# The state space branch's 256-column products: three products of high and low parts in place of one float32 product

## The chip, the cores and the metric

One core of one Trainium2 chip runs the whole program in one launch. The metric is the device time of that launch in microseconds (us). TensorE (PE) multiplies matrices, VectorE (DVE) and ScalarE (ACT) do the elementwise work, SyncE (SP) issues nearly all DMAs. Each engine takes its own instructions strictly in the order in which they were written for it, and waits at an instruction whose inputs, or whose buffer, are not ready.

## The reference

The model is two layers (sequence 512, width 1024, all float32). Each layer mixes tokens by three branches and then applies a gated MLP. The branch at issue is the Mamba-2 state space scan (16 heads of 64 channels in 4 groups, state 128, chunks of 128 tokens):

```python
cb = jnp.einsum('bctgn,bcsgn->bctsg', c, b)
y_diag = jnp.einsum('bctsg,bctsgh,bcsghp->bctghp', cb, decay, x)
states = jnp.einsum('bcsgn,bcsgh,bcsghp->bcghpn', b, to_end, x)
prev = chunk_prefix_states(jnp.exp(a_cum[:, :, -1])[..., None, None], states)
y_off = jnp.einsum('bctgn,bcghpn,bctgh->bctghp', c, prev, jnp.exp(a_cum))
return (y_diag + y_off).reshape(bsz, seq, nh, p)
```

For one group the heads' channels lie side by side, so `states` (B with x) and `y_off` (C with the states) are each one 128x128 by 128x256 product per chunk.

## The kernel before

All projections run as a stream of **units**. A unit is one 128x1024 tile of weights: SP loads it (`raw`), ACT casts it to the reduced type F32R (`wh`, L249), DVE forms the remainder (`wl`, L251), and PE does 24 matmuls of 512 columns with it (an F32R product is done three times: high by high, high by low, low by high, so that nearly float32 precision comes out). `wh` and `wl` have three buffers each, and the split is written three units ahead, so the cast of a unit waits until PE has finished the unit whose buffer it takes.

Everything else of the branches is written as Python generators (`side`), each resumed between units by `tick`, at the `yield`s it names. Their small matmuls go through `mm` and `transpose`, and after each small one `follow` puts one of the unit's 512-column matmuls. PE's order is the written one; ACT's and DVE's order, and the buffers, are set by a scheduler that reads the whole program at build time.

```python
def follow():
    if large:
        o, l, r, start, stop = large.popleft()
        PE.matmul(o, lhsT=l, rhs=r, start=start, stop=stop)     # L183

def mm(o, l, r, start, stop):
    PE.matmul(o, lhsT=l, rhs=r, start=start, stop=stop)         # L186
    follow()
```

A unit's matmuls that do not follow a small one are issued at L178. The names below: `xdt`, `xD`, `xe` are x times its step, its skip weight and its decay to the chunk's end (L833 to L836); `bt` is B transposed (L845); `cb` the masked product of C and B (L850); `M` the decay times `cb` (ACT L894 and L895, DVE L896); `prev` the running state (L873 to L877); `sy` the chunk's output, `jk` its square. `cx`, `cv`, `xbc` are the causal convolution and SiLU of a projection (DVE L771, ACT L773, DVE L775 three times, ACT L778, DVE L779). `th` and `mg` belong to the branch gates (DVE L918, ACT L919, DVE L943 and L945).

`ssd_group` runs once per group, four groups in two layers. In six steps, one per unit, it forms `M` for chunk 0 to 3 (steps 0 to 3) and does `chunk` for chunk 0 to 3 (steps 2 to 5). `chunk` issues four 64-column products of `M` with `xdt`, the product of C with `prev` (not for chunk 0), and the product of B with `xe` (not for chunk 3); DVE then makes the next `prev` from it. The next chunk, one unit later, needs that `prev`.

Of the kernel before, what the change touches and what calls it, by code (L numbers as in the profile page):

```python
# [12 lines left out]
F32R = mybir.dt.float32r  # L13
# [7 lines left out]
P = 128  # L21
# [115 lines left out]
def hybrid_decoder(ctx: ExitStack, tc: tile.TileContext, ins, out):  # L137
# [6 lines left out]
    def nm(s):  # L144
        ids[0] += 1
        return f"{s}_{ids[0]}"
# [10 lines left out]
    def big(shape, dt=F32, n="b"):  # L157
        return big_p.tile(shape, dt, tag="b", name=nm(n))
# [7 lines left out]
    def mx():  # L166
        return psum_p.tile([P, 512], F32, tag="ps", name=nm("mx"))

    V, A, PE = nc.vector, nc.scalar, nc.tensor
# [10 lines left out]
# [9 lines that stand above are left out]
    def transpose(o, i, idn):  # L189
        PE.transpose(o, i, idn)  # L190
        follow()
# [6 lines left out]
    def f(ap):  # L198
        return ap.bitcast(F32)
# [88 lines left out]
    def blk(c):  # L288
        return slice(c * P, (c + 1) * P)
# [514 lines left out]
    def bc4(ap):  # L804
        return ap.unsqueeze(2).to_broadcast([P, 4, 64])

    def ssd_group(l, g, dec, ch, zw, yh, yl):
        dt, acu, acr, e, dte = dec
        pc, rw = pcs[l], rows[l]
        bT, cT, x0, x1 = ch  # L810
        xg = big([P, 4, P], F32R, n="xg")
        V.tensor_mul(xg, f(acr).unsqueeze(1).to_broadcast([P, 4, P]),
                     own64[:, 4 * g:4 * g + 4].unsqueeze(2).to_broadcast([P, 4, P]))
        yield 1

        def hs(t, c):
            return t[:, c * 16 + 4 * g:c * 16 + 4 * g + 4]


        xdt, xd, xe = [], [], []  # L820
        for cc in range(2):
            o = mx()
            for c in range(2):
                for i, x in enumerate((x0, x1)):
                    transpose(o[:, 256 * c + P * i:256 * c + P * i + P], x[:, blk(2 * cc + c)], ident)
            td, tD, te = big([P, 2, 256], n="xdt"), big([P, 2, 256], n="xD"), big([P, 2, 256], n="xe")
            for c in range(2):
                ov = o[:, 256 * c:256 * c + 256].rearrange("p (h d) -> p h d", h=4)

                def v4(t):  # L830
                    return t[:, c].rearrange("p (h d) -> p h d", h=4)

                V.tensor_mul(v4(td), ov, bc4(hs(dt, 2 * cc + c)))  # L833
                V.tensor_mul(v4(tD), ov, bc4(rw[:, 32 + 4 * g:36 + 4 * g]))  # L834
                if 2 * cc + c < 3:
                    V.tensor_mul(v4(te), ov, bc4(hs(dte, 2 * cc + c)))  # L836
                xdt.append(td[:, c])
                xd.append(tD[:, c])
                xe.append(te[:, c])
        yield 1  # L840
        o = mx()
        for c in range(3):
            transpose(o[:, blk(c)], bT[:, blk(c)], ident)
        bt = big([P, 384], n="bt")
        A.copy(bt, o[:, :384])  # L845
        o = mx()
        for c in range(4):
            mm(o[:, blk(c)], bT[:, blk(c)], cT[:, blk(c)], True, True)
        cb = big([P, 4, P], n="cb")
        V.tensor_mul(cb, o.rearrange("p (c t) -> p c t", c=4), tri.unsqueeze(1).to_broadcast([P, 4, P]))  # L850
        ss = sml([P, 4], n="sss")
        ys = []

        def chunk(c, mt, prev):
            yd = mx()
            for h in range(4):
                mm(yd[:, 64 * h:64 * h + 64], mt[:, h], xdt[c][:, 64 * h:64 * h + 64], True, True)
            if c:
                mm(yd[:, 256:512], cT[:, blk(c)], prev, True, True)
            if c < 3:  # L860
                so = mx()
                mm(so[:, :256], bt[:, blk(c)], xe[c], True, True)
            y = big([P, 256], n="sy")
            V.tensor_add(y, yd[:, :256], xd[c])
            if c:
                t1 = big([P, 4, 64], n="t1")
                V.tensor_mul(t1, yd[:, 256:512].rearrange("p (h d) -> p h d", h=4), bc4(hs(e[:, 0], c)))
                V.tensor_add(y, y, t1.rearrange("p a b -> p (a b)"))
            nx = None
            if c < 3:  # L870
                nx = big([P, 256], n="prev")
                if c == 0:
                    V.tensor_copy(nx, so[:, :256])  # L873
                else:
                    V.tensor_mul(nx.rearrange("p (h d) -> p h d", h=4), prev.rearrange("p (h d) -> p h d", h=4),
                                 bc4(hs(e[:, 2], c)))
                    V.tensor_add(nx, nx, so[:, :256])  # L877
            V.scalar_tensor_tensor(y, y, hr[:, c:c + 1], zw[c], ALU.mult, ALU.mult)
            jk = big([P, 256], n="jk")
            A.activation(jk, y, AF.Square, accum_out=ss[:, c:c + 1])  # L880
            ys.append(y)
            return nx

        yield 1
        prev = None
        mts = []
        for c in range(6):
            if c < 4:
                sg = mx()
                mm(sg, own_c[:, c], xg.rearrange("p a b -> p (a b)"), True, True)  # L890
                mt = big([P, 4, P], n="M")
                for h in range(4):
                    j = 16 * c + 4 * g + h
                    A.activation(mt[:, h], sg[:, blk(h)], AF.Relu, bias=acu[:, j:j + 1], scale=-1.0)  # L894
                A.activation(mt, mt, AF.Exp, scale=-1.0)  # L895
                V.tensor_mul(mt, mt, cb[:, c:c + 1].to_broadcast([P, 4, P]))  # L896
                mts.append(mt)
            if c > 1:
                prev = chunk(c - 2, mts[c - 2], prev)
            yield 1  # L900
        V.tensor_scalar(ss, ss, 1.0 / 256.0, EPS, ALU.mult, ALU.add)
        ro = sml([P, 4], n="sro")
        rsqrt(ro, ss, 4)
        for c in range(4):
            A.activation(ys[c], ys[c], AF.Copy, scale=ro[:, c:c + 1])
        yield 2
        for i in range(2):
            o = mx()
            for c in range(4):
                transpose(o[:, blk(c)], ys[c][:, blk(i)], ident)  # L910
            split(yh[2 * g + i], yl[2 * g + i], o, pc[:, O_SNW + 2 * g + i:O_SNW + 2 * g + i + 1])
# [65 lines left out]
    for l in range(depth):  # L977
# [28 lines left out]
        for m in range(KD):  # L1006
            o = pp()
# [8 lines left out]
        for j in range(KF + 1):  # L1016
# [5 lines left out]
            if j:  # L1022
                i, og, ov = last
                s = big([P, T], n="fs")
                conv_silu(og, 3, lambda t: cw[:, 3 * i + t:3 * i + t + 1], cw[:, 66 + i:67 + i], s)()
                V.tensor_mul(s, s, ov)
                h, lo = big([P, T], F32R, n="hh"), big([P, T], F32R, n="hl")
# [7 lines left out]
        for m in range(KD):  # L1035
            o = pp()
            for k in range(KF):
# [3 lines left out]
                s = blk(idx % 8)  # L1041
# [89 lines left out]
```

## Time and profile before

| | |
|---|---|
| time, median of 3 runs | 2322.52 us (2321.18 to 2324.29) |
| the profiled execution | 2325.6 us, its span 2323.8 us |
| PE busy | 2300.8 us (99%) |
| DVE busy | 1420.4 us (61%) |
| ACT busy | 917.6 us (39%) |
| chain that ended last | PE 98%, DVE 1% |
| granted TensorE clock, mean | 0.995 |

The span runs from the first to the last instruction of the profiled execution; the time around it is what the launch adds. A busy share counts time in which the engine has an instruction at work. The chain that ended last is followed back from the last instruction, at each step to what released it.

### The profile page before, as it was taken

To read this page: it belongs to the slowest core of one execution; us is meant where nothing else is said; L and a number is where in the kernel's file an instruction comes from. 1 tells how busy PE (TensorE), PEld (TensorE's weight loads), DVE (VectorE), ACT (ScalarE), POOL (GpSimd) and SP (SyncE) were. 2 spreads that over 40 slices of the span, in tenths; PEclk is the share of its full clock that TensorE was granted. 3 is DMA by queue.
4 is the path that set the end of the run, shared out by engine and by line. 5 is a ranking of instruction groups with operands and counts; after the bars stand their busy time and mean duration, and the time that the engine had idled before them with its cause. 6 is when DMAs were issued, how large, how long until landed. Compare 5 with 4: busy or idle time off the path is not lost.

```text
span 2323.8 us, 27417 instructions
## 1 busy us (share of the span) xinstructions
PE 2300.8 (99%) x10776; PEld 1903.1 (82%) x10776; DVE 1420.4 (61%) x2527; ACT 917.6 (39%) x1503; POOL 0.2 (0%) x4
## 2 busy tenths in 40 slices
PE   8999999999999999999999999999999999999997
PEld 7888878888888888888888888788888888888886
DVE  5467548687865566654335764686888556665533
ACT  5354423445443333332244444234454433333321
POOL 0000000000000000000000000000000000000000
PEclk9999999999999999999999999999999999999998
DMA  5322222222223333333333222222222233323331
GB/s 182 105 77 82 73 64 87 78 72 73 82 73 100 92 99 95 96 100 94 97 91 100 83 82 73 71 84 73 73 73 82 82 95 96 97 94 100 98 93 54
DMA packets 58512, 204.21 MB, mean 88 GB/s; under 512 B 7152, under 2 KB 7824, under 8 KB 58384
## 3 DMA queue, kind: packets, MB, share of 16 engines
q1 hardware_dynamic: 57808, 201.42, 28.8%
q8 instruction: 84, 1.38, 0.2%
q10 hardware_dynamic: 576, 1.05, 0.1%
q14 instruction: 44, 0.36, 0.1%
HBM read 200.35 MB, written 2.10 MB: 87 GB/s over the span
## 4 chain that ended last, share of the span: by engine, by line
PE 98%; DVE 1%; ACT 0%; DMA 0%; issue 0%; DVEq 0%; SPq 0%; ACTq 0%
PE pp L178 77%; PE pp L183 11%; PE mx L186 8%; PE mx L190 2%; DVE wl L251 0%; DVE x L1069 0%; DVE cv L775 0%; DMA x<-in_xT 0%; DVE xD L834 0%; DVE th L918 0%; DVE th L943 0%; DVE xdt L833 0%; DVE xe L836 0%; ACT cx L778 0%; ACT L350 0%
## 5 line engine op out<-in xcount | busy, mean ns | idle before, releaser
L249 ACT CAST wh<-raw 128x1024 fp32r<-128x1024 f32 x374 | 393.1, 1051 | 952.7 <-PE pp L178 727.9
L251 DVE TENSOR_TENSOR wl<-raw,wh 128x1024 fp32r<-128x1024 f32 x374 | 457.4, 1223 | 355.6 <-ACT wh L249 350.1
L178 PE MATMUL pp<-xh,wl 128*128 128x512 f32 x1582 | 617.7, 390 | 0.0
L178 PE MATMUL pp<-xl,wh 128*128 128x512 f32 x1556 | 607.0, 390 | 0.0
L178 PE MATMUL pp<-xh,wh 128*128 128x512 f32 x1504 | 587.8, 391 | 0.0
L178 PEld LDWEIGHTS pp<-xh,wl 128*128 128x128 f32 x1582 | 297.7, 188 | 63.5 <-issue 1.0
L178 PEld LDWEIGHTS pp<-xl,wh 128*128 128x128 f32 x1556 | 293.1, 188 | 60.5 <-issue 0.5
L178 PEld LDWEIGHTS pp<-xh,wh 128*128 128x128 f32 x1504 | 283.3, 188 | 60.4 <-DVE wl L251 1.5
L183 PE MATMUL pp<-xh,wh 128*128 128x512 f32 x304 | 148.3, 488 | 0.0
L178 PE MATMUL pp<-hh,wl 128*128 128x512 f32 x352 | 136.9, 389 | 0.0
L178 PE MATMUL pp<-hh,wh 128*128 128x512 f32 x352 | 136.9, 389 | 0.0
L178 PE MATMUL pp<-hl,wh 128*128 128x512 f32 x352 | 136.9, 389 | 0.0
L771 DVE TENSOR_TENSOR cx<-pp,rstdB 128x512 f32<-128x512 f32 x76 | 52.3, 689 | 121.1 <-PE pp L178 121.0
L183 PE MATMUL pp<-xl,wh 128*128 128x512 f32 x252 | 124.6, 495 | 0.0
L183 PE MATMUL pp<-xh,wl 128*128 128x512 f32 x226 | 111.4, 493 | 0.0
L178 PE MATMUL pp<-wh,xh 128*128 128x512 f32 x245 | 96.3, 393 | 7.9 <-ACT wh L249 7.9
L178 PE MATMUL pp<-wh,xl 128*128 128x512 f32 x264 | 103.4, 392 | 0.0
L778 ACT ACTIVATE cx<-cv 128x512 f32<-128x512 f32 x76 | 48.1, 632 | 139.6 <-DVE cv L775 138.8
L178 PE MATMUL pp<-wl,xh 128*128 128x512 f32 x258 | 101.2, 392 | 0.5 <-DVE wl L251 0.5
L178 PE MATMUL pp<-wh,xr 128*128 128x512 f32 x255 | 78.7, 389 | 0.0
L178 PEld LDWEIGHTS pp<-hl,wh 128*128 128x128 f32 x352 | 66.1, 188 | 13.8
L178 PEld LDWEIGHTS pp<-hh,wl 128*128 128x128 f32 x352 | 66.1, 188 | 13.7
(275 smaller groups left out, 3542.6 us busy)
## 6 DMA issues: line engine op xcount, KB each, us to landing
raw<-in_wall SPq DMA_DIRECT2D x374, 512.0 KB, 3.6
x<-in_xT SPq DMA_DIRECT2D x8, 256.0 KB, 6.0
out_dram<-x ACTq DMA_DIRECT2D x4, 256.0 KB, 2.3
out_dram<-x SPq DMA_DIRECT2D x4, 256.0 KB, 2.5
cosR<-in_rope SPq DMA_DIRECT2D x2, 256.0 KB, 4.6
sinR<-in_rope SPq DMA_DIRECT2D x2, 256.0 KB, 4.8
amask<-in_amask SPq DMA_DIRECT2D x1, 256.0 KB, 5.3
levf<-in_lev SPq DMA_DIRECT2D x1, 224.0 KB, 3.7
```

The source lines that it names most:

```text
L178: PE.matmul(o, lhsT=l, rhs=r, start=start, stop=stop)
L183: PE.matmul(o, lhsT=l, rhs=r, start=start, stop=stop)
L186: PE.matmul(o, lhsT=l, rhs=r, start=start, stop=stop)
L190: PE.transpose(o, i, idn)
L249: A.copy(h, r)
L251: V.tensor_sub(lo, r, f(h))
L771: V.tensor_mul(x, o, rstdB)
L778: A.activation(x, v, AF.Tanh)
```

## The change

The operands of the two 256-column products become pairs of F32R tiles: a high part (ACT copy) and a low part (DVE difference). Each product becomes three. `parted` makes a pair, `three` issues the three matmuls.

```diff
+    def parted(src, n, name):
+
+        h, lo = big([P, n], F32R, n=name), big([P, n], F32R, n=name)
+        A.copy(h, src)
+        V.tensor_sub(lo, src, f(h))
+        return h, lo
+
+    def three(o, l, s, r):
+        mm(o, l[0][:, s], r[0], True, False)
+        mm(o, l[0][:, s], r[1], False, False)
+        mm(o, l[1][:, s], r[0], False, True)
...
-                xe.append(te[:, c])
+            n = 512 if cc == 0 else 256
+            h, l = parted(te.rearrange("p c d -> p (c d)")[:, :n], n, "xe")
+            xe += [(h[:, i:i + 256], l[:, i:i + 256]) for i in range(0, n, 256)]
...
-        bt = big([P, 384], n="bt")
-        A.copy(bt, o[:, :384])
+        bt = parted(o[:, :384], 384, "bt")
+        cp_ = parted(cT[:, P:], 384, "cT")
...
             if c:
-                mm(yd[:, 256:512], cT[:, blk(c)], prev, True, True)
+                three(yd[:, 256:512], cp_, blk(c - 1), prevs[-1])
             if c < 3:
                 so = mx()
-                mm(so[:, :256], bt[:, blk(c)], xe[c], True, True)
+                three(so[:, :256], bt, blk(c), xe[c])
...
+                prevs.append(parted(nx, 256, "prev"))
```

In the changed kernel's rows L810 and L811 are the copy and the difference in `parted`; L878, L881, L889, L882, L891, L893 and L895 are the old L864, L867, L875, L868, L877, L878 and L880; L909 to L911 the old L894 to L896; L933, L934 and L958 the old L918, L919 and L943.

**First place: the first group of a layer, ACT.** The rows run from the cast of one unit to the exponential of the first `M`, before the change:

```order
L249 CAST wh_4097<-raw_3907 128x1024
L773 ACTIVATE cv_4040<-cx_4038,scw_2599 128x512
L845 COPY bt_4059<-mx_4052 128x384
L249 CAST wh_4139<-raw_3964 128x1024
L778 ACTIVATE cx_4038<-cv_4040 128x512
L894 ACTIVATE M_4104<-mx_4101,acu_2905 128x128 x4
L919 ACTIVATE th_4092<-th_4092 128x512
L895 ACTIVATE M_4104<-M_4104 128x512
```

The same stretch of the changed kernel (`wh_4153` is the cast that was `wh_4139`, `M_4118` the tile that was `M_4104`):

```order
L249 CAST wh_4111<-raw_3907 128x1024
L810 CAST xe_4010<-xe_4003 128x512
L810 CAST xe_4031<-xe_4025 128x256
L249 CAST wh_4153<-raw_3964 128x1024
L773 ACTIVATE cv_4048<-cx_4046,scw_2599 128x512
L810 CAST bt_4067<-mx_4060 128x384
L810 CAST cT_4071<-xbc_3576 128x384
L778 ACTIVATE cx_4046<-cv_4048 128x512
L249 CAST wh_4205<-raw_4054 128x1024
L909 ACTIVATE M_4118<-mx_4115,acu_2905 128x128 x4
L934 ACTIVATE th_4106<-th_4106 128x512
L910 ACTIVATE M_4118<-M_4118 128x512
```

Three casts are new. The cast of one unit moved ahead of the convolution's step `cv` and of `bt`, and the cast of the next unit moved ahead of `M`; before, that one stood after the second `M`.

**The same place on DVE**, from the low part of the unit's weights to the first `M`, before:

```order
L251 TENSOR_TENSOR wl_4141<-raw_3964,wh_4139 128x1024
L775 SCALAR_TENSOR_TENSOR cv_4040<-cx_4038,scw_2599,cv_4040 128x509
L779 SCALAR_TENSOR_TENSOR xbc_4037<-cx_4038,cv_4040 128x512
L918 TENSOR_TENSOR th_4092<-pp_4045,rstdB 128x512
L918 TENSOR_TENSOR th_4135<-pp_4094,rstdB 128x512
L943 SCALAR_TENSOR_TENSOR th_4092<-th_4092,pp_4143 128x512
L896 TENSOR_TENSOR M_4104<-M_4104,cb_4070 128x512
```

and after:

```order
L251 TENSOR_TENSOR wl_4155<-raw_3964,wh_4153 128x1024
L775 SCALAR_TENSOR_TENSOR cv_4048<-cx_4046,scw_2599,cv_4048 128x511
L811 TENSOR_TENSOR bt_4068<-mx_4060,bt_4067 128x384
L775 SCALAR_TENSOR_TENSOR cv_4048<-cx_4046,scw_2599,cv_4048 128x510
L811 TENSOR_TENSOR cT_4072<-xbc_3576,cT_4071 128x384
L775 SCALAR_TENSOR_TENSOR cv_4048<-cx_4046,scw_2599,cv_4048 128x509
L864 TENSOR_TENSOR cb_4084<-mx_4075,mats 128x512
L779 SCALAR_TENSOR_TENSOR xbc_4045<-cx_4046,cv_4048 128x512
L933 TENSOR_TENSOR th_4106<-pp_4053,rstdB 128x512
L933 TENSOR_TENSOR th_4149<-pp_4108,rstdB 128x512
L251 TENSOR_TENSOR wl_4207<-raw_4054,wh_4205 128x1024
L911 TENSOR_TENSOR M_4118<-M_4118,cb_4084 128x512
```

Behind `wl_4155` stand now all three steps of the convolution, `cb`, two low parts and the low part of the next unit, before `M` comes; the first two steps and `cb` stood ahead of that `wl` before.

**Second place: the third state of a layer's second group, DVE**, before the change:

```order
L867 TENSOR_TENSOR t_920_4663<-mx_4647,dec_2899 128x256
L875 TENSOR_TENSOR prev_4666<-prev_4585,dec_2899 128x256
L868 TENSOR_TENSOR sy_4661<-sy_4661,t_920_4663 128x256
L877 TENSOR_TENSOR prev_4666<-prev_4666,mx_4658 128x256
L878 SCALAR_TENSOR_TENSOR sy_4661<-sy_4661,hr,zw_3472 128x256
L251 TENSOR_TENSOR wl_4697<-raw_4465,wh_4695 128x1024
```

and after:

```order
L775 SCALAR_TENSOR_TENSOR cv_4679<-cx_4677,scw_2599,cv_4679 128x509
L878 TENSOR_TENSOR sy_4735<-mx_4713,xD_4278 128x256
L881 TENSOR_TENSOR t_944_4737<-mx_4713,dec_2899 128x256
L889 TENSOR_TENSOR prev_4740<-prev_4651,dec_2899 128x256
L882 TENSOR_TENSOR sy_4735<-sy_4735,t_944_4737 128x256
L891 TENSOR_TENSOR prev_4740<-prev_4740,mx_4728 128x256
L893 SCALAR_TENSOR_TENSOR sy_4735<-sy_4735,hr,zw_3472 128x256
L251 TENSOR_TENSOR wl_4771<-raw_4517,wh_4769 128x1024
L811 TENSOR_TENSOR prev_4744<-prev_4740,prev_4743 128x256
```

On ACT the high part of that state (`prev_4743`) is written behind the unit's cast `wh_4769` and the convolution's tanh:

```order
L350 ACTIVATE ysh_2583<-mx_4691,pc_92 128x512
L350 ACTIVATE ysh_2584<-mx_4702,pc_92 128x512
L249 CAST wh_4769<-raw_4517 128x1024
L778 ACTIVATE cx_4677<-cv_4679 128x512
L810 CAST prev_4743<-prev_4740 128x256
```

PE needed only the sum `prev_4666` before; it needs both parts now, and the low part stands behind a 128x1024 difference.

**Third place: the second state of a layer's third group, DVE**, after the change (`scw` stands there in the first layer alone):

```order
L891 TENSOR_TENSOR prev_5311<-prev_5311,mx_5299 128x256
L911 TENSOR_TENSOR M_5277<-M_5277,cb_5073 128x512
L893 SCALAR_TENSOR_TENSOR sy_5306<-sy_5306,hr,zw_4507 128x256
L765 TENSOR_SCALAR scw_11466<-pc_95 128x80
L251 TENSOR_TENSOR wl_5341<-raw_5154,wh_5339 128x1024
L811 TENSOR_TENSOR prev_5315<-prev_5311,prev_5314 128x256
```

Here too the low part of the state stands behind a unit's `wl`. At the other states the low part stands ahead of the next `wl` or a unit's length before its use.

## Rows read from the trace of the kernel before

**Rows 1.** The page: engines' busy time, share of the span and instructions; then the chain that ended last, by engine.
```profile
PE 2300.8 (99%) x10776; PEld 1903.1 (82%) x10776; DVE 1420.4 (61%) x2527; ACT 917.6 (39%) x1503; POOL 0.2 (0%) x4
...
PE 98%; DVE 1%; ACT 0%; DMA 0%; issue 0%; DVEq 0%; SPq 0%; ACTq 0%
```

**Rows 2.** Who waited for whom, PE's own waits: total us, times, longest.
```profile
PE mx L186 <- DVE M L896: 1.4, 2, 0.7
```

**Rows 3.** PE's groups by shape: operation, output and inputs, shapes, count, busy us, mean ns of one. A float32 matmul is two instructions.
```profile
L186 PE MATMUL mx<-xe,bt 128*128 128x256 f32 x48 | 14.2, 377 | 0.0
...
L186 PE MATMUL mx<-prev,xbc 128*128 128x256 f32 x48 | 14.2, 377 | 0.0
```

**Rows 4.** From the page's costliest groups, the weight loads of the projections: mean ns of one.
```profile
L178 PEld LDWEIGHTS pp<-xh,wl 128*128 128x128 f32 x1582 | 297.7, 188 | 63.5 <-issue 1.0
```

**Rows 5.** PE's timeline at the second group's third and fourth chunk: start us, duration us, line, output and inputs, shape, instructions merged. Seven more L178 rows stand between 565.82 and 567.64, each 0.22 to 0.24 after the one before.
```profile
564.26 0.59 PE L186 MATMUL mx<-prev,xbc 128*128 128x256 f32 x2
...
564.92 0.59 PE L186 MATMUL mx<-xe,bt 128*128 128x256 f32 x2
...
565.82 0.39 PE L178 MATMUL pp<-xh,wh 128*128 128x512 f32 x1
...
567.64 0.39 PE L178 MATMUL pp<-xh,wl 128*128 128x512 f32 x1
567.87 0.33 PE L186 MATMUL mx<-xdt,M 128*128 128x64 f32 x2
...
569.68 0.59 PE L186 MATMUL mx<-prev,xbc 128*128 128x256 f32 x2
```

**Rows 6.** PE's timeline, other small matmuls between 512-column ones, in the same columns: transposes, then float32 products of 128 columns.
```profile
525.53 0.27 PE L190 MATMUL mx<-mats,xbc 128*128 128x128 f32 x1
...
525.87 0.27 PE L190 MATMUL mx<-mats,xbc 128*128 128x128 f32 x1
...
526.55 0.38 PE L186 MATMUL mx<-xbc,xbc 128*128 128x128 f32 x2
...
527.00 0.38 PE L186 MATMUL mx<-xbc,xbc 128*128 128x128 f32 x2
```

**Rows 7.** ACT's timeline ahead of the first layer's first chunk, in the same columns; in brackets the idle time before and what ended it.
```profile
507.21 1.05 ACT L249 CAST wh<-raw 128x1024 fp32r<-128x1024 f32 x1 [0.76 <-PE pp L178]
510.27 0.63 ACT L778 ACTIVATE cx<-cv 128x512 f32<-128x512 f32 x1 [2.01 <-DVE cv L775]
510.81 1.12 ACT L894 ACTIVATE M<-mx,acu 128x128 f32<-128x128 f32 x4
512.26 0.63 ACT L919 ACTIVATE th<-th 128x512 f32<-128x512 f32 x1 [0.33 <-DVE th L918]
512.80 0.61 ACT L895 ACTIVATE M<-M 128x512 f32<-128x512 f32 x1
```

**Rows 8.** DVE's timeline at the same place, and last the PE row that waited for it.
```profile
506.29 0.74 DVE L775 SCALAR_TENSOR_TENSOR cv<-cx,scw,cv 128x511 f32<-128x511 f32 x1
506.95 0.68 DVE L850 TENSOR_TENSOR cb<-mx,mats 128x512 f32<-128x512 f32 x1
507.55 0.73 DVE L775 SCALAR_TENSOR_TENSOR cv<-cx,scw,cv 128x510 f32<-128x510 f32 x1
508.29 1.23 DVE L251 TENSOR_TENSOR wl<-raw,wh 128x1024 fp32r<-128x1024 f32 x1
509.44 0.74 DVE L775 SCALAR_TENSOR_TENSOR cv<-cx,scw,cv 128x509 f32<-128x509 f32 x1
...
513.53 0.68 DVE L896 TENSOR_TENSOR M<-M,cb 128x512 f32<-128x512 f32 x1
...
514.27 0.43 PE L186 MATMUL mx<-xdt,M 128*128 128x64 f32 x2 [0.72 <-DVE M L896]
```

**Rows 9.** The second place, two units around the third state of the second group: ACT's rows, then DVE's.
```profile
561.01 0.80 ACT L773 ACTIVATE cv<-cx,scw 128x512 f32<-128x512 f32 x1
...
567.84 1.05 ACT L249 CAST wh<-raw 128x1024 fp32r<-128x1024 f32 x1 [1.87 <-PE pp L178]
...
560.72 1.23 DVE L251 TENSOR_TENSOR wl<-raw,wh 128x1024 fp32r<-128x1024 f32 x1 [0.15 <-ACT wh L249]
...
564.51 0.74 DVE L775 SCALAR_TENSOR_TENSOR cv<-cx,scw,cv 128x509 f32<-128x509 f32 x1
...
566.50 0.41 DVE L877 TENSOR_TENSOR prev<-prev,mx 128x256 f32<-128x256 f32 x1
566.83 0.47 DVE L878 SCALAR_TENSOR_TENSOR sy<-sy,hr,zw 128x256 f32<-128x256 f32 x1
```

**Rows 10.** The third place, around the second state of the third group: PE's rows, then one of ACT.
```profile
631.06 0.33 PE L186 MATMUL mx<-xdt,M 128*128 128x64 f32 x2
...
632.88 0.59 PE L186 MATMUL mx<-prev,xbc 128*128 128x256 f32 x2
...
631.03 1.05 ACT L249 CAST wh<-raw 128x1024 fp32r<-128x1024 f32 x1 [1.57 <-PE pp L178]
```

**Rows 11.** PE's timeline in the second layer where the clock fell; the last row is the sum over a stretch (from:to, length, then busy us of PE, weight loads, DVE, ACT and POOL, then PEclk, the granted clock, where 1.00 is 2.4 GHz, then DMA).
```profile
1476.66 0.63 PE L178 MATMUL pp<-xh,wh 128*128 128x512 f32 x1
...
1479.22 0.51 PE L178 MATMUL pp<-xh,wh 128*128 128x512 f32 x1
...
1474.00:1478.00 4.00, 4.00 (x13) 2.65 (x13) 0.76 (x3) 0.00 (x0) 0.00 (x0) 0.76 0.00 0
```

More of the change, by code (lines that the diff above doesn't have):

```diff
@@ L851, in ssd_group @@
         ss = sml([P, 4], n="sss")
-        ys = []
+        ys, prevs = [], []
         def chunk(c, mt, prev):
```

## The prediction

> **What bounds the kernel now.** I read the page first. PE is busy for 99% of the span, and the chain that ended last lies on it for 98%, while DVE is busy for 61% and ACT for 39% [rows 1]. So what PE saves is time, and work on ACT and DVE costs only what it makes PE wait. The view of the waits says where that is near: among PE's own waits stands the one for `M` (DVE, L896), twice, the longest 0.7 us [rows 2]. The timeline there shows PE at 514.27 after 0.72 us of idling [rows 8]; it is the first `M` of a layer, once in each layer, and so a place without any slack. Last I read the timeline around the 256-column products. Each float32 product is two instructions; there are 48 instructions for each of the two sorts [rows 3], so 24 products each, 48 in all.
>
> **What PE saves.** From 564.26 to 564.92 PE does one float32 256-column product and one 512-column product: 0.66 us. A 512-column product alone is (567.64 - 565.82) / 8 = 0.2275 us [rows 5]. The float32 product costs 0.66 - 0.2275 = 0.43 us.
>
> In its place stand three F32R products of 256 columns, and the trace has none of that shape. The bound from below is half of a 512-column product, 0.1138 us, less what such a product may have of fixed cost: I put 0.107 there. The nearest rows for a small product between large ones are a transpose, 525.87 - 525.53 - 0.2275 = 0.11, and a float32 product of 128 columns, which passes twice: (527.00 - 526.55 - 0.2275) / 2 = 0.111 a pass [rows 6]. With some hundredths of the reading of starts in hundredths, 0.12 is the bound from above. I take 0.116, so three cost 0.348 and the gain is 0.086 us a product, 48 x 0.086 = 4.1 us. The bounds give 48 x 0.07 = 3.6 and 48 x 0.11 = 5.3 us.
>
> The change also raises these products' weight loads, from 96 to 144, one for each instruction. A load takes 188 ns by its row [rows 4], while 512-column products follow each other every 0.2275 us, so those loads lie beside the products before them; I cost them at nothing, hidden by the large product that follows each small one. A small product of 0.11 us hides less than a load of 0.19; if the load behind each of the 144 small ones showed its rest, 0.188 - 0.116 = 0.07 us, that would cost 144 x 0.07 = 10.4 us. Against it speak the same transposes and 128-column passes, whose loads are as large and which cost 0.11.
>
> The Trainium skill speaks against the change here: its page "TensorE: Matmul & The Clock Gate", section "Part 3: Packing small matmuls", says that a weight load overlaps matmuls in flight only when the row group differs, and all rows here use all 128 partitions. The trace disagrees, since 188 ns of load and a whole 512-column product would not fit into 0.2275 us. By the rule each of the 48 added loads would stand open, an estimated 9 us by the 0.188 of its row; I give that no more than the chance of the costlier products below.
>
> **What ACT and DVE get.** For each group: casts and differences of `xe` (512 and 256 columns), `bt` (384, its cast in the place of the copy), `cT` (384) and three `prev` (256 each). On DVE a 256-column step takes 0.33 us from start to start (566.50 to 566.83) [rows 9], a 512-column one 0.60 (`cb`, 506.95 to 507.55), a step of the convolution 0.66 (506.29 to 506.95), a unit's `wl` 1.15 (508.29 to 509.44) [rows 8]; for 384 I estimate 0.47, between 0.33 and 0.60. A group gets some 3 us on each engine, over six units of about 7 us. Most of it is hidden behind PE's work: where I followed the written order, operands were ready 2 to 4 us early. Three places are not covered, and both layers have them in the same order, so each counts twice.
>
> **First place, `M` of the first group.** ACT's cast of the unit, released by PE at 507.21 [rows 7], now stands ahead of `cv` and `bt`, and the `wl` ahead of the three convolution steps. So DVE runs `wl` from 508.31, and behind it `cv` 509.45, the low part of `bt` 510.11, `cv` 510.58, the low part of `cT` 511.24, the last `cv` 511.71. That one ends at 512.45; it ended at 509.44 + 0.74 = 510.18 before. The tanh (L778) therefore starts at 512.50 in place of 510.27. Behind it ACT now has the next unit's cast, 1.05 us with 0.95 to the next start as instructions overlap by 0.1: that stood behind the second `M`. So the four exponents of `M` (about 1.0 us; 1.12 by their row) start at 513.98, the tanh of `th` at 514.98 and the exponential of `M` at 515.50, and it ends 0.61 us later, at 516.13 [rows 7]. DVE has done `cb`, `xbc`, two `th` and the next `wl` by 516.12, so `M` starts at 516.18, and PE, 0.74 behind it as in 513.53 to 514.27, at 516.91 [rows 8]. That is 2.64 us later than before: PE would idle for 3.4 us. Queued behind the waiting product are all later products of PE, so nothing covers it. Twice: 5.3 us. If the orders ahead slip less than I read, the least is nothing.
>
> **Second place, the third state of the second group.** Before, DVE had the sum at 566.50 + 0.41 = 566.91, and PE wanted it at 569.68 [rows 5, 9]. Its `wl` at 560.72 starts 0.17 earlier, two products' gain, at 560.55. Behind it stand now the low part of the state before, `xbc` and `cx`, until 560.55 + 1.15 + 0.33 + 2 x 0.60 = 563.2, ending 563.3; ACT's `cv`, 0.80 long, ran from 561.01 before and now ends at 564.17. Then DVE has three convolution steps with two 512-column steps between, 2 x 0.66 + 2 x 0.60 + 0.74 = 3.3, to 567.5 (565.25 before, 564.51 + 0.74). Four steps of 256 columns and the sum's own 0.41 later, the sum ends at 569.24. ACT's cast follows from 569.3 to 569.7. PE, which by then has saved 0.38 us, would take the high part at 569.30 and takes it at 569.75: 0.45 us. The low part stands behind `sy` and a `wl` of 1.15 us and ends at 571.1; PE wants it one small and one large product after the high one, at 569.75 + 0.34 = 570.09, and has it at 571.15: 1.06 us. Together 1.5, in two layers 3.0 us.
>
> **Third place, the second state of the third group.** The unit begins at U = 631.06, its cast at U - 0.03 [rows 10]. The `wl` starts some 0.03 behind the cast's end, the low part 1.15 later, and that takes 0.41, so PE can have it at about U - 0.03 + 1.05 + 0.03 + 1.15 + 0.41 + 0.05 = U + 2.66. The high product starts at U + 1.82 (631.06 to 632.88) and the low part is wanted 0.34 later, at U + 2.16: 0.5 us, twice 1.0.
>
> **The sum.** -4.1 + 5.3 + 3.0 + 1.0 = +5.2 us. The profiled execution took 2325.6 us, 3.1 (0.13%) above the median of 2322.5, its span 2323.8 and 1.8 us around it. It becomes 2330.8, on the median's basis 2327.7, rounded 2328, +0.2%. What a measurement of this kernel can tell from no change is 0.2%, 4.65 us, so the forecast lies just above that bound.
>
> **The rivals.**
>
> *The clock falls in the new gap.* In the second layer the clock was at 1.2 GHz for a while though PE did not idle, only did small products: 13 in 4 us, mean granted clock 0.76, and a 512-column product took 0.63 us, at 1479.22 still 0.51, against 0.39 [rows 11]. PE idles longer at the first place, 3.4 us, and the clock might fall too. The slow rows there reach from 1476.66 to 1479.22, and with a product on either side I put such a spell at 3.4 us; in it products come every 0.43 us, twice 0.2275, so 8 of them lose 8 x 0.2 = 1.6 us. For both layers this gives +8.4 us, 2331. It hangs on a gap as long as I work out; a much shorter one speaks against it, since with gaps of 0.7 us [rows 2] PE kept its pace.
> The Trainium skill, page "TensorE: Matmul & The Clock Gate", section "Why this matters for your kernels", warns that an idle gap between bursts of matmuls sends the clock back to half. No stretch of this trace has such a gap in the middle of the work, so it neither agrees nor disagrees.
>
> *The waits are hidden, and the time doesn't rise* (the other side). All three places rest on orders that I walked by hand with durations of before. Some rows for it: the first `M` hangs on the tanh, and if the cast of the unit is released earlier or the convolution's steps run ahead of `wl`'s release, it loses only the cast's 0.95 us. Then PE's 48 x 0.086 us stand against 2 x 0.95 and some of the 4 us of the other places: from -4.1 to +2 us, 2319 to 2324. It decides from where the first place loses under 1.5 us a layer. Below -4.65 us, faster by what can be told, it takes both no wait and products of under 0.112 us ((0.434 - 4.65 / 48) / 3): possible, but the order puts the low part of `prev` behind `wl` at two places.
>
> *Small products cost more.* If the rest of each load shows, the 10.4 us from above come on top: +15.6, 2338. If a 256-column F32R product cost a float32 pass, 0.43 / 2 = 0.217 us, three would cost 0.65 and the 48 products lose 10.4 in place of gaining 4.1: +20, 2342. The passes of 128 columns at 0.11 speak against both. Waits that I missed, at 4 to 8 us, would end at the same place: a group has 13 more tiles in the shared pool, whose reuse I followed by the order alone.
>
> **How the numbers follow.** The forecast (three places, clock kept) gets 0.38, the clock's rival 0.34, hidden waits 0.18, costlier products or more waits 0.10. The forecast's own spread, from the product's price and a place more or less, is +3 to +7 us; some four tenths of it lie below 4.65, so it gives 0.22 slower and 0.16 the same. The clock's rival gives 0.31 slower and 0.03 the same, the hidden waits 0.05 faster and 0.13 the same, the last 0.09 slower and 0.01 the same. That is faster 0.05, same 0.33, slower 0.62. The range: from 2320.5, which leaves out the lower third of the hidden waits, to 2335, which takes in the clock's rival with one more wait and leaves out most of the last; under 2 in 10 is outside.
>
> **What would show it.** The gain: in the changed trace the 256-column F32R products start 0.11 to 0.12 us before the next large one. First place: PE waits for `M` (L911), twice, some 3.4 us each, near 514 and at the same place of the second layer, and the tanh at L778 starts some 2 us later. Second and third: PE rows of L186 that wait for L810 and L811 of `prev`, 1.5 and 0.5 us a layer. The clock: the granted clock in a window behind the first place, 1.00 or about 0.5. The prediction is wrong if PE doesn't wait for L911 beyond 1.5 us, or if the small products cost over 0.13 us.

## The result and the profile after

The changed kernel takes 2337.26 us (median of 6 runs, 2336.1 to 2339.59) against 2323.08 of the kernel before (6 runs beside them): 1.0064 of it, 95% interval 1.0052 to 1.0076. That is +14.2 us, slower as forecast, but nearly three times the +5.2 of the sum and above the range. The profiled execution has a span of 2337.8 us, 14.0 more than before, so its trace holds the whole difference.

The page's engines (busy us, share of the span, instructions) and the chain by engine; [rows 1] are the same rows of before:

```profile
PE 2306.5 (99%) x10824; PEld 1907.1 (82%) x10824; DVE 1445.3 (62%) x2583; ACT 939.0 (40%) x1551; POOL 0.2 (0%) x4
...
PE 97%; DVE 2%; ACT 1%; issue 0%; DMA 0%; DVEq 0%; SPq 0%; ACTq 0%
```

PE has 48 more instructions, DVE 56 and ACT 48. DVE is busy 25 us more and ACT 21; on shares of a whole span nothing looks dangerous. PE's own waits (us in total, times, longest) show where it hurts; [rows 2] had 1.4 us for the first `M`:

```profile
PE mx L186 <- DVE M L911: 6.6, 2, 3.3
...
PE mx L186 <- DVE prev L811: 2.3, 4, 0.8
...
PE mx L190 <- DVE xD L846: 0.7, 2, 0.4
...
PE mx L186 <- ACT prev L810: 0.4, 2, 0.2
```

These waits are 8.6 us more than before. PE's timeline at the first place shows what the waits don't; [rows 8] end with the same product before, at 514.27:

```profile
512.88 0.47 PE L183 MATMUL pp<-wh,xh 128*128 128x512 f32 x1
516.66 0.69 PE L186 MATMUL mx<-xdt,M 128*128 128x64 f32 x2 [3.31 <-DVE M L911]
517.11 0.78 PE L183 MATMUL pp<-wl,xh 128*128 128x512 f32 x1
517.69 0.52 PE L186 MATMUL mx<-xdt,M 128*128 128x64 f32 x2
517.97 0.77 PE L183 MATMUL pp<-wh,xl 128*128 128x512 f32 x1
...
523.45 0.28 PE L190 MATMUL mx<-mats,xbc 128*128 128x128 f32 x1
```

Behind the gap of 3.31 us everything PE does lasts longer: a pair with a 64-column product takes 0.86 us (517.11 to 517.97), and such a pair took 0.46 before (514.51 to 514.97 in the same view). The windows of that stretch name the reason (from:to, length, busy us of PE, weight loads, DVE, ACT and POOL, then PEclk, DMA share and GB/s):

```profile
516.00:518.00 2.00, 1.34 (x6) 1.24 (x6) 2.00 (x4) 2.00 (x7) 0.00 (x0) 0.66 0.48 84
518.00:520.00 2.00, 2.00 (x8) 1.81 (x9) 2.00 (x4) 1.63 (x5) 0.00 (x0) 0.50 0.44 178
520.00:522.00 2.00, 2.00 (x7) 1.70 (x7) 1.17 (x4) 0.00 (x0) 0.00 (x0) 0.50 0.00 0
522.00:524.00 2.00, 2.00 (x9) 1.40 (x8) 1.22 (x3) 0.90 (x3) 0.00 (x0) 0.63 0.00 0
524.00:526.00 2.00, 2.00 (x13) 1.58 (x12) 1.89 (x6) 0.00 (x0) 0.00 (x0) 1.00 0.00 0
```

From 516.66 to 523.45, for 6.8 us, TensorE ran at 0.50 of its speed, 1.2 GHz. The rival of the clock came true, in both layers, and twice as long as the 3.4 us that it was given.

### The profile page after: what moved, and what is told of

It reads as the page before. It is cut to its first block, busy times and chain, and to the rows that moved or that the text cites. A ratio compares the mean times of both kernels' runs of the same rounds, so it can differ in the third digit from the quotient of the medians.

```text
span 2337.8 us, 27625 instructions
## 1 busy us (share of the span) xinstructions
PE 2306.5 (99%) x10824; PEld 1907.1 (82%) x10824; DVE 1445.3 (62%) x2583; ACT 939.0 (40%) x1551; POOL 0.2 (0%) x4
## 4 chain that ended last, share of the span: by engine, by line
PE 97%; DVE 2%; ACT 1%; issue 0%; DMA 0%; DVEq 0%; SPq 0%; ACTq 0%
PE pp L178 76%; PE pp L183 12%; PE mx L186 8%; PE mx L190 1%; DVE wl L251 1%; ACT wh L249 0%; DVE cv L775 0%; DVE x L1084 0%; DMA x<-in_xT 0%; DVE ysl L351 0%; DVE th L933 0%; DVE prev L811 0%; ACT cv L773 0%; DVE M L911 0%; DVE xe L811 0%
## 5 line engine op out<-in xcount | busy, mean ns | idle before, releaser
L178 PE MATMUL pp<-xh,wl 128*128 128x512 f32 x1564 | 610.6, 390 | 0.0
L178 PE MATMUL pp<-xl,wh 128*128 128x512 f32 x1532 | 597.6, 390 | 0.0
L178 PE MATMUL pp<-xh,wh 128*128 128x512 f32 x1482 | 579.0, 391 | 0.0
L178 PEld LDWEIGHTS pp<-xh,wl 128*128 128x128 f32 x1564 | 294.3, 188 | 62.2 <-issue 1.0
L178 PEld LDWEIGHTS pp<-xl,wh 128*128 128x128 f32 x1532 | 288.5, 188 | 59.4 <-issue 0.5
L178 PEld LDWEIGHTS pp<-xh,wh 128*128 128x128 f32 x1482 | 279.2, 188 | 59.7 <-DVE wl L251 1.5
L178 PE MATMUL pp<-hh,wl 128*128 128x512 f32 x352 | 136.9, 389 | 0.0
L178 PE MATMUL pp<-hh,wh 128*128 128x512 f32 x352 | 136.9, 389 | 0.0
L178 PE MATMUL pp<-hl,wh 128*128 128x512 f32 x352 | 136.9, 389 | 0.0
L178 PE MATMUL pp<-wh,xh 128*128 128x512 f32 x237 | 93.2, 393 | 7.6 <-ACT wh L249 7.6
L178 PE MATMUL pp<-wh,xl 128*128 128x512 f32 x256 | 100.4, 392 | 0.0
L178 PE MATMUL pp<-wl,xh 128*128 128x512 f32 x250 | 98.2, 393 | 0.5 <-DVE wl L251 0.5
L178 PE MATMUL pp<-wh,xr 128*128 128x512 f32 x255 | 78.7, 389 | 0.0
L775 DVE SCALAR_TENSOR_TENSOR cv<-cx,scw,cv 128x511 f32<-128x511 f32 (+2 forms) x96 | 71.7, 747 | 9.7 <-ACT cv L773 8.7
L178 PEld LDWEIGHTS pp<-hh,wl 128*128 128x128 f32 x352 | 66.1, 188 | 13.8
```

The lines of the kernel that those rows point to most:

```text
L775: V.scalar_tensor_tensor(v[:, i:], x[:, :T - i], w(width - 1 - i), v[:, i:], ALU.mult, ALU.add)
```

## The experiments

To compare traces I pair the 512-column products of the projections, of which every kernel here has the same 8976 in the same order, and follow by how much each starts later. Steps in that shift, by place, are called shifts below.

**What the gap does to the clock.** Theory A says that the idle gap itself lowers the clock; rival B that the short products around it do. The first run fills the gap and leaves the rest as it is:

```diff
             yd = mx()
+            if g == 0 and c == 0:
+                for _ in range(13):
+                    PE.matmul(yd, lhsT=own_c[:, 0], rhs=xg.rearrange("p a b -> p (a b)"), start=True, stop=True)
```

> The changed kernel with one addition: while PE would wait for the first M of a layer, it does 13 F32R products of 512 columns into the bank that the M products then overwrite (their result is thrown away). 13 x 0.2275 = 2.96 us of the 3.31 us gap are filled, and ACT and DVE have the same order. Theory A: the idle gap lowers the clock. Then the clock stays at 1.00 behind the gap, some 3.2 us a layer come back, and the time is 14.2 - 6.4 = about +8 us over the kernel before. Rival B: the fall comes from what PE does there (short products with half-empty columns, or the F32R ones of 256 columns), and the gap only stands beside it. Then the clock falls all the same and the time stays at +14.

It took 2332.09 us against 2323.01, ratio 1.0042 (1.0027 to 1.0057). PE's timeline there, and then a window behind it:

```profile
514.12 3.29 PE L872 MATMUL mx<-xg,own_c 128*128 128x512 f32 x13 [0.88 <-DVE th L936]
517.25 0.33 PE L186 MATMUL mx<-xdt,M 128*128 128x64 f32 x2
517.38 0.48 PE L183 MATMUL pp<-wl,xh 128*128 128x512 f32 x1
```

```profile
518.00:520.00 2.00, 2.00 (x14) 1.78 (x14) 2.00 (x4) 1.49 (x5) 0.00 (x0) 1.00 0.30 121
```

The products of the kernel still start 3 us late, but at the full clock: the shift over the first place is 3.3 us in place of 5.8 and 5.5. The thrown-away work had to wait 0.88 us for its bank, and so ended somewhat late. It saved 5 us of 14.

The counterpart makes the gap in the kernel before, which has none of the new products:

```diff
                 A.activation(mt, mt, AF.Exp, scale=-1.0)
+                if g == 0 and c == 0:
+                    for _ in range(2):
+                        V.tensor_max(mt, mt, mt)
                 V.tensor_mul(mt, mt, cb[:, c:c + 1].to_broadcast([P, 4, P]))
```

> The kernel before, float32 products, with two maxima of M with itself (512 columns, values unchanged) ahead of the first M of a layer on DVE. By the order two other steps slip in between, so that M comes 4 x 0.6 = 2.4 us later and the gap is 0.7 + 2.4 = 3.1 us. Theory A: the clock falls behind it as in the changed kernel, and the time rises by 2 x (2.4 + 3.2) = +11 us. Rival B: without the new products the clock stays at 1.00, and the time rises by 2 x 2.4 = +4.8 us.

2332.17 us, ratio 1.0038 (1.0023 to 1.0052). Its timeline and a window:

```profile
516.41 0.66 PE L186 MATMUL mx<-xdt,M 128*128 128x64 f32 x2 [3.22 <-DVE M L899]
516.83 0.77 PE L183 MATMUL pp<-wl,xh 128*128 128x512 f32 x1
```

```profile
518.00:520.00 2.00, 2.00 (x8) 1.71 (x8) 2.00 (x4) 0.00 (x0) 0.00 (x0) 0.50 0.35 33
```

With float32 products the clock falls just as it does in the changed kernel. The shift is 5.5 us in the first layer and 5.1 in the second, of which 2.5 are the gap. So B is out: a gap of 3.2 us is enough by itself. The same edit with `range(1)`:

> The same with one maximum and, by the order, one step between: M comes 1.2 us later, a gap of about 1.9 us. Theory A, with a fall that needs a long gap: the clock holds, +2.4 us. If a gap of this length is already enough: 2 x (1.2 + 3.2) = +9 us.

2326.32 us, ratio 1.0014 (1.0005 to 1.0024), and after the shorter gap PE keeps its pace in the traced execution, in both layers (timeline and window of the first):

```profile
513.10 0.41 PE L186 MATMUL mx<-xdt,M 128*128 128x64 f32 x2 [2.00 <-ACT M L895]
513.31 0.48 PE L183 MATMUL pp<-wl,xh 128*128 128x512 f32 x1
```

```profile
513.00:515.00 2.00, 1.90 (x13) 1.76 (x14) 2.00 (x4) 2.00 (x6) 0.00 (x0) 1.00 0.00 0
```

Here 1.3 us more of idling cost 1.3 us a layer; in the run before 2.5 us cost 5.3. The traced execution took 2324.33 us, and the ten of this kernel reach up to 2330.64, 4.8 us above the highest of the kernel before beside them (2325.86), where two longer gaps explain 2.5. So it is not shown that the clock holds behind a gap of 2.0 us every time, and where between 2.0 and 3.0 us the one turns into the other was not tried.

**What the products give.** No work is added; the written edit is this, and `xe`, `bt`, C and `prev` become F32R tiles:

```diff
     def parted(src, n, name):
-        h, lo = big([P, n], F32R, n=name), big([P, n], F32R, n=name)
-        A.copy(h, src)
-        V.tensor_sub(lo, src, f(h))
-        return h, lo
+        return src, src
```

> The three F32R products of the change, with no work added on ACT and DVE: the tiles are written as F32R at once, and the high part stands in for the low one, so the low parts are left out of the computation and this run tells the price of the products alone. By the prediction (0.116 us a product) -4.1 us. By the changed kernel's rows, where six such products and six large ones take 2.13 us (538.37 to 540.50), a product costs (2.13 - 6 x 0.2275) / 6 = 0.1275, three 0.38, and the gain is 0.05 x 48 = -2.4 us. If the products themselves lowered the clock (rival B): +4 us and more.

2320.81 us, ratio 0.9989 (0.998 to 0.9998), 2.2 us faster. From the first place on the shift against the kernel before is -1.5 us in each layer, -0.06 for each of 24 products, 2.9 in all. PE waits for `M` as before, and the other steps of this shift lie outside the branch (the start of the program and two stretches that the last section deals with), so this trace is the base for the account below.

**Which work makes `M` late.** First all casts and differences, with the float32 products (`bf` and `xf` are the undivided copies):

```diff
-                three(yd[:, 256:512], cp_, blk(c - 1), prevs[-1])
+                mm(yd[:, 256:512], cT[:, blk(c)], prev, True, True)
...
-                three(so[:, :256], bt, blk(c), xe[c])
+                mm(so[:, :256], bf[:, blk(c)], xf[c], True, True)
```

> All casts and differences of the change are made, but PE keeps the two float32 products, so the parts are computed and not used (the output is that of the kernel before). If it is the added work on ACT and DVE that makes the first M late: a gap of about 3.3 us at the first place, the clock falls behind it, no wait for parts of the state, and the time is 2 x (2.6 + 3.1) = +11.4 us, +12.5 with the wait for xD in the second group. If the products on PE make the loss: about +0.

2335.12 us against 2323.13, +12.0, ratio 1.0054 (1.004 to 1.0067). PE waits for `M` twice for 3.0 us, and for `xD` twice for 1.1. The loss is made without a single new product.

Then each half. Only B with x: as the changed kernel without `cp_` and the parts of `prev`, and with the float32 product of C.

> Only the product of B with x is split (xe and bt in parts); C with the states stays float32. By the order ACT has the next unit's cast ahead of M here too. So the gap at the first place should stay, 3.3 us with the clock's fall, 11.3 us in two layers, less 24 x 0.06 = 1.5 us for the products, and no wait for a state: +10 us. If the low part of C (cT) is what makes M late: +2 us or less.

2332.83 us, +9.7, ratio 1.0043 (1.0029 to 1.0057). Only C with the states: `xe` and `bt` as before the change, `cp_` and `prev` in parts.

> Only the product of C with the states is split (cT and prev in parts); B with x stays float32. By the order the next unit's cast stands behind the second M as in the kernel before. So the first place should keep its gap of 0.7 us and the clock; the second place keeps its waits for the low part of prev (1.6 us a layer), the third has no wl in the way: 3.2 - 1.5 = +1.7 us. If any added cast at the first place costs the long gap: +11 us and more.

2324.28 us, +1.2, ratio 1.0005 (0.9996 to 1.0014). PE's waits in the two halves, B with x first:

```profile
PE mx L186 <- DVE M L909: 7.0, 2, 3.5
```

```profile
PE mx L186 <- DVE prev L811: 1.6, 2, 0.8
...
PE mx L186 <- DVE M L910: 0.5, 2, 0.2
```

Each half brings its own wait. The long gap comes with the half that splits `xe`, though the other half, too, adds a cast and a difference at that place. The remaining question is whether it is the work or its place in the order. The same half with the parts of `xe` written three units later (on ACT the first of them then starts at 510.75 us in place of 502.69):

```diff
-            n = 512 if cc == 0 else 256
-            h, l = parted(te.rearrange("p c d -> p (c d)")[:, :n], n, "xe")
-            xe += [(h[:, i:i + 256], l[:, i:i + 256]) for i in range(0, n, 256)]
+            tes.append(te)
...
                 mts.append(mt)
+            if c == 1:
+                for n, t in zip((512, 256), tes):
+                    h_, l_ = parted(t.rearrange("p c d -> p (c d)")[:, :n], n, "xe")
+                    xe.extend([(h_[:, i:i + 256], l_[:, i:i + 256]) for i in range(0, n, 256)])
```

> As e6_bx, only B with x split, with one move: the parts of xe are made behind the second M of a group, so that by the order the casts of the weights stand as in the kernel before. If it is the place of xe's casts, and nothing else of this half, that made the first M late: a gap of 0.24 us (as in e8_late) in place of 3.5, no fall of the clock there, no waits for a state, and -1.5 - 1.0 = -2.5 us against the kernel before, 0.1% faster. If the work itself is too much for these units: a new wait elsewhere, and 0 to +3 us.

2321.66 us against 2323.26, ratio 0.9992 (0.9983 to 1.0001). ACT's timelines around the first `M`, with the casts early (e6_bx) and late (e11_bx_late):

```profile
507.42 1.05 ACT L249 CAST wh<-raw 128x1024 fp32r<-128x1024 f32 x1 [1.34 <-PE pp L178]
...
512.87 0.63 ACT L778 ACTIVATE cx<-cv 128x512 f32<-128x512 f32 x1 [3.32 <-DVE cv L775]
513.40 1.03 ACT L249 CAST wh<-raw 128x1024 fp32r<-128x1024 f32 x1
514.34 1.13 ACT L907 ACTIVATE M<-mx,acu 128x128 f32<-128x128 f32 x4
```

```profile
504.13 1.05 ACT L249 CAST wh<-raw 128x1024 fp32r<-128x1024 f32 x1 [0.76 <-PE pp L178]
506.42 0.63 ACT L778 ACTIVATE cx<-cv 128x512 f32<-128x512 f32 x1 [1.24 <-DVE cv L775]
506.96 1.12 ACT L905 ACTIVATE M<-mx,acu 128x128 f32<-128x128 f32 x4
```

Counted from the weight cast ahead of it, the tanh comes after 5.45 us with the casts early and after 2.29 with the casts late, and then no weight cast stands between it and `M`. PE's gap for `M` is 0.24 us, shorter than before the change, and no new wait appears. Same work, 11 us apart: it was the order. The point estimate of -1.6 us (0.08%) is just short of what this measurement tells from no change, and it is the only version here beside e4_products that measured below the kernel before.

**The states.** The whole change with the parts of `xe` and C made late, as in the run above, and in a chunk:

```diff
-            if c:
-                three(yd[:, 256:512], cp_, blk(c - 1), prevs[-1])
             if c < 3:
                 so = mx()
                 three(so[:, :256], bt, blk(c), xe[c])
+            if c:
+                s, p = blk(c - 1), prevs[-1]
+                mm(yd[:, 256:512], cp_[0][:, s], p[0], True, False)
+                mm(yd[:, 256:512], cp_[1][:, s], p[0], False, False)
+                mm(yd[:, 256:512], cp_[0][:, s], p[1], False, True)
```

> The whole change with three moves in the written order: the parts of xe and of C are made behind the second M of a group, a chunk does B with x ahead of C with the state, and the low part of the state is multiplied last (some 1.4 us later than now). By the order the first M stands on ACT and DVE as in the kernel before. If the three places and the clock are the whole loss, only the products' gain stays: a gap of 0.7 us at the first place, no waits for prev, about -2.9 us against the kernel before. If there is a further cost of the change that the waits do not show (loads, buffers), the time is that of the kernel before or above it.

2323.92 us against 2323.13, ratio 1.0003 (0.9994 to 1.0012). The first place is mended (a gap of 0.24 us, clock 1.00), and 13 of the 14 us are gone. But the second place waits longer than in the changed kernel, where it was 0.22 and 0.82 us:

```profile
568.03 0.39 PE L186 MATMUL mx<-prev,cT 128*128 128x256 f32 x1 [0.95 <-ACT prev L810]
...
569.46 0.39 PE L186 MATMUL mx<-prev,cT 128*128 128x256 f32 x1 [0.46 <-DVE prev L811]
```

My expectation had a mistake in it: this is the fourth chunk of a group, which has no product of B with x, so there the new order gains 0.35 us and not 1.4. Two more runs put eight of the unit's large products in front, the first in the changed kernel, the second in e8_late for the fourth chunk alone:

```diff
+                for _ in range(8):
+                    follow()
                 three(yd[:, 256:512], cp_, blk(c - 1), prevs[-1])
```

> The changed kernel, with eight of the unit's 512-column products put ahead of each product of C with the state, so that PE wants the state 8 x 0.2275 = 1.8 us later. If the waits at the second and third place are as the changed kernel's trace has them (1.6 and 0.6 us a layer, the lost overlap included), these 4.4 us go, the first place keeps its gap and the clock's fall, and the time is about +9.6 us over the kernel before. If the low part only waits longer (DVE as the bound of these units): +12 us or more.

> The run with the three moves (e8_late), and beside them eight 512-column products ahead of the product of C with the last state of a group, where that run still has PE wait 0.95 and 0.46 us in the second group. With these gone, some 1.9 us a layer by its steps, only the products' gain of 2.9 us and a shorter first gap (0.24 for 0.72 us, 1.0 us in two layers) are left: -3.5 to -4 us, 0.17% under the kernel before. Rival: as e8_late, within 1 us of it, since the wait moves with DVE.

2336.19 us (+12.9, ratio 1.0057, 1.0042 to 1.0072) and 2323.87 us (+0.6, ratio 1.0003, 0.9995 to 1.0012): both came out as the rival had it. The waits moved. In e9_states PE still waits twice for a low part, 0.8 us, and now for the group's output, and in e10_both four times for a low part:

```profile
PE mx L190 <- ACT sy L922: 2.6, 2, 1.3
...
PE mx L186 <- DVE prev L811: 1.6, 2, 0.8
```

```profile
PE mx L186 <- DVE prev L811: 1.6, 4, 0.4
```

When PE asks for a state later, DVE gets that chunk's results later, and its order is planned anew around them; that this is the reason is argued and not tested. By the shifts, the places behind the first cost 3.0 us a layer in e9_states and 2.8 in the changed kernel. In the three orders with the first place mended (e7_cs, e8_late, e10_both) the waits for the state cost 1.7 to 2.0 us a layer, where its 12 products save 0.7. So the split of the states costs more than it saves in each of them, and eats what the other half gains; whether some order exists that frees it is open.

## Why the prediction was right and wrong

Each place as a shift of the changed kernel against e4_products, beside the sum's term (us, one layer):

| term | forecast | first layer | second layer |
|---|---|---|---|
| products, 24 | -2.05 | -1.5 | -1.4 |
| first place, the wait | +2.64 | +2.6 | +2.6 |
| first place, the clock | 0 (rival: 1.6) | +3.2 | +2.9 |
| second group, `xD` | none | +0.55 | +0.54 |
| second place, third state | +1.5 | +1.57 | +1.59 |
| third place | +0.5 | +0.61 | +0.62 |

The products' row is e4_products against the kernel before. The wait is 3.31 - 0.72 = 2.59, and the clock is the rest of the 5.8 and 5.5 us. The columns add up to +13.9; measured +14.2.

**The walk through the orders: right.** All three waits came where they were forecast and at their size. ACT's and DVE's rows at the first place, behind [rows 7] and [rows 8], have the tanh, the inserted cast and `M`:

```profile
512.23 0.64 ACT L778 ACTIVATE cx<-cv 128x512 f32<-128x512 f32 x1 [2.77 <-DVE cv L775]
512.77 1.03 ACT L249 CAST wh<-raw 128x1024 fp32r<-128x1024 f32 x1
513.71 1.14 ACT L909 ACTIVATE M<-mx,acu 128x128 f32<-128x128 f32 x4
...
515.92 0.69 DVE L911 TENSOR_TENSOR M<-M,cb 128x512 f32<-128x512 f32 x1
```

The walk had 512.50, 513.03, 513.98 and 516.18, and the rows stand some 0.27 earlier throughout, since this execution reached the place 0.30 us ahead of the one before. The second place, too, is as walked (0.45 and 1.06 of waiting; 0.22 and 0.82 of idling in the trace, and the rest below):

```profile
575.51 0.38 PE L186 MATMUL mx<-prev,cT 128*128 128x256 f32 x1 [0.22 <-ACT prev L810]
575.73 0.39 PE L183 MATMUL pp<-xl,wh 128*128 128x512 f32 x1
576.94 0.39 PE L186 MATMUL mx<-prev,cT 128*128 128x256 f32 x1 [0.82 <-DVE prev L811]
```

**The step that failed: the clock.** The forecast let PE idle for 3.4 us and priced only the idling; the fall behind it stood as a rival with 0.34 against 0.38. e1_filler and e2_gap show that the gap alone does it, so with a gap of that length the rival was the likelier case, and it was not two cases but one. It was also mis-sized: I took the length of the slow spell from [rows 11], 3.4 us; behind the gap it lasted 6.8 us, and its price was 3.0 us a layer, not 1.6. With that term the sum would have been +11.3. Both lengths exist (last section), and the trace of before had both: the stretch from 325 to 333 us, shown there, holds one of the longer sort. Where a run has the short spell behind the gap, the step costs what the rival gave it: in e9_states the first layer's shift there is 4.25 us, 1.7 more than the longer gap explains, and the second layer's, with the long spell, 5.45.

The trace of before also has gaps with a slow clock behind them, at the program's end: PE idles there for 1.38 and 3.34 us, and the granted clock is 0.74 from 2306 to 2312 us and 0.50 from there on. The prediction set them aside as not in the middle of the work; PE does only ten matmuls behind the first of them, so they don't separate the gap from the little work around it.

**The products: right in sign, mis-sized.** Six of them with six large ones take 2.13 us in the changed trace, 0.1275 each by that reading and (0.4325 - 0.06) / 3 = 0.124 by the shifts, above my upper bound of 0.12:

```profile
538.37 0.28 PE L186 MATMUL mx<-prev,cT 128*128 128x256 f32 x1
538.49 0.40 PE L183 MATMUL pp<-wl,xh 128*128 128x512 f32 x1
538.72 0.28 PE L186 MATMUL mx<-prev,cT 128*128 128x256 f32 x1
...
540.14 0.28 PE L186 MATMUL mx<-xe,bt 128*128 128x256 f32 x1
540.26 0.40 PE L183 MATMUL pp<-wh,xh 128*128 128x512 f32 x1
540.50 0.39 PE L186 MATMUL mx<-xg,own_c 128*128 128x512 f32 x1
```

The nearest rows had 128 columns, or two passes of 128; I took them for the bound of a shape that streams twice as long. The sign that I named came true, a start 0.11 to 0.12 us before the next large product; the rest of the price lies behind the large ones, where the next start comes up to 0.24 us later. So the gain is 2.9 us and not 4.1. (Of the bounds, 48 x 0.07 is 3.4 and not 3.6.) The loads stay hidden for the most part: a product costs 0.1275 with its load, and a load alone lasts 0.188. The rule on weight loads of the Trainium skill ("TensorE: Matmul & The Clock Gate", "Part 3: Packing small matmuls"), by which the added ones would have cost an estimated 9 us, is not what this trace shows: the 48 added instructions came with a gain.

**The wait that I missed.** In the second group the transposes wait 0.36 us for `xD`, 0.55 us a layer in the shift: PE's next bank is read by DVE, which is behind. That was one of the "more waits" of the last rival, at a quarter of its price.

**The range.** Without the clock's spell the time would have been +8, and so in the range. Its top, 2335, was the clock's rival with one more wait of some 4 us. The spells cost 6.1 us in place of the rival's 3.2, the products gave 1.2 less than forecast, and the wait that I missed took 1.1. With the short spell in both layers the sum would have been 13.9 - 6.1 + 2 x 1.65 = +11.1, inside the range; nothing that I had read told which of the two lengths would follow.

## What to carry to other kernels

Where a gap of PE grows, price the idling and the slow work behind it together: here 2.5 us more of idling cost 5.3 us, while 1.3 us more cost 1.3 in the execution that was traced. Before work is added to engines that look 40% and 62% busy, follow what a scheduler does with the order at the place with the least slack: in the half with B and x, the same casts written three units later took the whole loss away. A state that is carried from step to step and needs both a high and a low part puts two more handovers into its loop, and moving its use later moved the wait without removing it.

## What had not been expected of the hardware

**A wait costs more than its idling.** At the second place PE idles for 0.22 + 0.82 = 1.04 us and loses 1.57; at the third 0.34 and 0.61; before the transposes 0.36 and 0.55. Products overlap: a 512-column one lasts 0.39 us and the next starts 0.23 behind it, so a wait of up to 0.16 us would show no idling at all. The four waits here cost 0.19 to 0.27 us each beside the idling that they show.

**The clock's spells come and go between executions of the same code.** The 64-row products of the first layer's other branch ran from 325 to 333 us at 0.57 of the clock in the kernel before, and at 1.00 in e3_short_gap, whose instructions are the same there:

```profile
325.00:333.00 8.00, 8.00 (x22) 5.27 (x21) 0.96 (x3) 0.00 (x0) 0.00 (x0) 0.57 0.00 0
```

```profile
325.00:333.00 8.00, 8.00 (x32) 5.15 (x31) 1.70 (x6) 1.38 (x2) 0.00 (x0) 1.00 0.03 11
```

By the shift that is 2.9 us between two executions, with another 1.6 us at the same place of the second layer. It is the likely source of the spread of a kernel's runs (2320.0 to 2325.8 for the kernel before), and of e2_gap's median lying below the sum of its two gaps; it was not tested by itself. Behind the long gap, too, the spell has no one length. It lasted 6.8 us in both layers of the changed kernel and nearly as long in e2_gap, but some 3.4 us in e6_bx, whose gap is 3.5 us, and in e5_work, whose gap is 3.0. In e9_states both lengths stand in one trace, behind gaps of 3.3 us in the first layer (product for `M` at 514.57) and in the second (1666.05); the windows begin 3.4 us behind each:

```profile
518.00:520.00 2.00, 2.00 (x13) 1.67 (x12) 1.87 (x5) 0.44 (x2) 0.00 (x0) 0.90 0.00 0
1669.50:1671.50 2.00, 2.00 (x7) 1.57 (x7) 1.17 (x4) 0.00 (x0) 0.00 (x0) 0.50 0.00 0
```

So it is not the kernel that sets the length. What decides between the two is open. The Trainium skill, "TensorE: Matmul & The Clock Gate", "Why this matters for your kernels", warns of idle gaps between bursts. The runs here agree: the clock fell at all ten gaps of 3.0 to 3.5 us in the traces of five kernels, and at neither of the two of 2.0 us that were traced. It also fell while PE was fully busy, as the rows of 325 to 333 us show.
